# A decoder trunk on one core: new costs in the kernel's own scheduler, another load order in a pair, fewer warm-up matmuls

## The chip, the core and the metric

The kernel runs on one core of a Trainium2 chip. The metric is the device time of one execution in microseconds, median of the runs shown. The program is built in Python: it first plans the order of all its instructions on the host and then issues them in that order, each engine's queue in order. Only the time on the device counts.

## What is computed

A trunk of two decoder layers on 256 positions of width 1024, in float32. Each layer has a SwiGLU feed-forward block, a mixer (a chunkwise mLSTM in the first layer, differential attention on shared keys and values in the second), a second SwiGLU block and a gated input embedding; RMS norms stand around each of them. Cut to what matters:

```python
def reference(x, p, norm_g, w_ffn_in, w_ffn_out, ...):
    for layer in range(DEPTH):                      # 2
        g = norm_g[layer]
        h = swiglu(rms_norm(x, g[0]), w_ffn_in[layer, 0], w_ffn_out[layer, 0])
        x = x + 0.5 * rms_norm(h, g[1])
        h = rms_norm(x, g[2])
        h = mlstm_mixer(h, ...) if layer < N_A_LAYERS else diff_attention(h, k_sh, v_sh, ...)
        x = x + rms_norm(h, g[3])
        h = swiglu(rms_norm(x, g[4]), w_ffn_in[layer, 1], w_ffn_out[layer, 1])
        x = x + 0.5 * rms_norm(h, g[5])
        gate = jax.nn.sigmoid(rms_norm(x, g[6]) @ w_ple_gate[layer])
        x = x + rms_norm((p[layer] @ w_ple_proj[layer]) * gate, g[7])
        if layer == N_A_LAYERS - 1:
            k_sh, v_sh = shared_kv(x, kv_norm, w_kv)
    return x
```

`swiglu` is `(silu(gate) * up) @ w_out` with `gate, up = split(x @ w_in)`; its hidden width is 2816, worked on as 11 slices of 256 (`NJ`).

## The kernel before

**Arithmetic.** A float32 product is made from three products of TensorE's faster float32r type. `split` writes a high part of a tile with ScalarE (`activation` Copy to float32r) and the remainder with VectorE (`tensor_tensor` subtract); `mm3` then multiplies high by high, high by low and low by high. Weights arrive as raw tiles of 128 x 2048 float32, 1 MB each (`wraw`, 8 buffers), and are split into `whi` and `wlo` (6 buffers each). The 256 positions are two row tiles, t = 0 and 1.

**Pairs.** Within a feed-forward block some slices are taken two at a time (`PAIRS`, 15 pairs in all; one more is in the mLSTM). `block_pair` works out the 2 x 2 block product of (two row tiles) by (two slices) with seven block products in place of eight, in Strassen's manner, with sums and differences of weight tiles. Its function `load` issues a plain load on SP's queue and, for a sum, a second load on GpSimd's queue that adds into the same tile (`accum_op`). A pair takes seven transfers: `t3` (two), `u1` (two), `b11`, `b21` and `b22`. VectorE adds `b11 + t3` and `b21 + b11` (`add`, into the raw tiles). TensorE uses the parts in the order `w11`, `w21`, `wt2`, `wu1`, `wt3`, `w22`, `wt4`.

**The hidden chain.** For each slice and row tile `hidden` does a SiLU (ScalarE, tile `sg`), a product (VectorE, `h`), two transposes (TensorE, `tr`), and a split (`hh`, `hl`); `stage_out` multiplies the result with the output weights into `accO`. At the end of a block `post` forms the norm: squares on ScalarE (`waste`), two small operations on GpSimd (`sm`), then the update of `x` on VectorE.

**The planner.** The kernel is recorded twice. In the first recording `Notes.add` notes each operation with what it must follow; `Notes.cost` gives it `dur` (how long its engine is taken) and `lat` (when its result is there). `Notes.play` then plays the program event by event: it keeps a clock for each engine and, for each engine, chooses among the operations that could start first, by their rank (place in the program) and whether they are marked urgent (the splits of weights are not). Buffers of a tag are given out in program order as they become free. SP takes the lowest rank of those loads that have a buffer, with at most eight loads (`LANES`) in flight. The result, `self.order`, is the order in which the second recording issues everything (`issue`, line 389, which is why every row of the profile names L389). The chip's engines then run their queues in that fixed order and wait for what they need by semaphores; the planned times decide only the order.

For the costs before: a plain load begins 1.9 us after its issue, runs at 400 bytes a ns after the load before it, and is there 0.4 us later. An accumulating load begins 4 us after its issue, runs at 165 bytes a ns, holds up plain loads for the same time, and is there 4 us later. An operation of VectorE costs 155 ns beside its elements, one of ScalarE 200 (172 from PSUM), with the results 50 and 40 ns later.

**Start.** While the first loads are on their way, TensorE runs 12 matmuls on a zero tile (line 506).

## Time and profile before

| what | value |
|---|---|
| median of 3 runs | 1011.77 us |
| runs | 1009.74 to 1012.2 us |
| the profiled execution's own time | 1012.75 us |
| its span, first to last instruction | 1011.0 us |
| mean granted TensorE clock | 0.998 |
| moved by DMA | 262.11 MB, 259 GB/s over the span |

How to read the rows below. PE is TensorE's matmuls, PEld its weight loads, DVE VectorE, ACT ScalarE, POOL GpSimd and SP SyncE, which only issues loads; a q behind a name is the engine's sequencer. A group's row gives line, engine, operation, the tiles written and read (buffer numbers left out), the shape, the count, then busy time, mean ns of one, and idle time of the engine just before them with what ended it. In the timeline a row has start, duration, engine, operation, and in square brackets the idle time before it. The end of a matmul is modelled: neighbours overlap in the records, and the distance between two starts is the true pace.

### The profile page before, as it was taken

To read this page: it belongs to the slowest core of one execution; us is meant where nothing else is said; L and a number is where in the kernel's file an instruction comes from. 1 tells how busy PE (TensorE), PEld (TensorE's weight loads), DVE (VectorE), ACT (ScalarE), POOL (GpSimd) and SP (SyncE) were. 2 spreads that over 40 slices of the span, in tenths; PEclk is the share of its full clock that TensorE was granted. 3 is DMA by queue.
4 is the path that set the end of the run, shared out by engine and by line. 5 is a ranking of instruction groups with operands and counts; after the bars stand their busy time and mean duration, and the time that the engine had idled before them with its cause. 6 is when DMAs were issued, how large, how long until landed. Compare 5 with 4: busy or idle time off the path is not lost.

```text
span 1011.0 us, 12465 instructions
## 1 busy us (share of the span) xinstructions
PE 996.6 (99%) x4692; PEld 815.2 (81%) x4692; DVE 847.1 (84%) x886; ACT 674.3 (67%) x909; POOL 77.3 (8%) x118
## 2 busy tenths in 40 slices
PE   9999999999999999999999999999999999999997
PEld 7887787888878888888887888778778888888786
DVE  6999895888879899987888898986985899999783
ACT  7666683667657767656875677766866767768372
POOL 0000000100121000001110000000101200000010
PEclk9999999999999999999999999999999999999999
DMA  9999974955699788765779998784556997897631
GB/s 341 395 308 296 306 279 152 279 206 198 247 318 277 251 290 263 282 257 172 292 259 327 321 300 301 240 322 170 201 217 235 311 263 235 293 303 269 229 124 43
DMA packets 44132, 262.11 MB, mean 259 GB/s; under 512 B 5288, under 2 KB 5672, under 8 KB 15912
## 3 DMA queue, kind: packets, MB, share of 16 engines
q1 hardware_dynamic: 39176, 227.50, 58.7%
q0 software_dynamic: 4608, 33.56, 17.1%
q8 instruction: 37, 0.61, 0.2%
q10 hardware_dynamic: 288, 0.27, 0.1%
q14 instruction: 23, 0.19, 0.1%
HBM read 250.82 MB, written 10.49 MB: 258 GB/s over the span
## 4 chain that ended last, share of the span: by engine, by line
PE 83%; DMA 7%; DVE 6%; issue 2%; ACT 1%; POOL 0%; SPq 0%; DVEq 0%; POOLq 0%; ACTq 0%
PE accI L389 51%; PE accO L389 28%; DMA wraw<-in_ffn_in 5%; PE tr L389 4%; DVE wraw L389 1%; DVE wlo_4r L389 1%; DMA wraw<-in_x 1%; DVE wlo_3r L389 1%; DMA wraw<-in_xT 1%; DMA att<-in_diff_lambda 1%; DVE wlo_2r L389 1%; DVE wlo_1r L389 1%; DVE att L389 1%; DVE wlo_5r L389 0%; DVE sm L389 0%
## 5 line engine op out<-in xcount | busy, mean ns | idle before, releaser
L389 ACT ACTIVATE whi_0r<-wraw 128x2048 fp32r<-128x2048 f32 (+2 forms) x51 | 74.9, 1477 | 17.1 <-PE accI L389 4.9
L389 ACT ACTIVATE whi_1r<-wraw 128x2048 fp32r<-128x2048 f32 (+2 forms) x52 | 74.7, 1449 | 9.5 <-DMA wraw<-in_ffn_in 3.8
L389 ACT ACTIVATE whi_5r<-wraw 128x2048 fp32r<-128x2048 f32 (+1 forms) x49 | 72.6, 1493 | 9.5 <-DMA wraw<-in_ffn_in 2.5
L389 ACT ACTIVATE whi_2r<-wraw 128x2048 fp32r<-128x2048 f32 (+1 forms) x45 | 70.2, 1571 | 9.3 <-DMA wraw<-in_ffn_in 5.8
L389 ACT ACTIVATE whi_3r<-wraw 128x2048 fp32r<-128x2048 f32 (+1 forms) x47 | 72.2, 1546 | 5.4 <-PE accI L389 2.6
L389 ACT ACTIVATE whi_4r<-wraw 128x2048 fp32r<-128x2048 f32 (+1 forms) x44 | 69.8, 1599 | 8.5 <-DMA wraw<-in_ffn_in 3.4
L389 DVE TENSOR_TENSOR wraw<-wraw,wraw 128x2048 f32<-128x2048 f32 x32 | 73.0, 2282 | 0.1
L389 ACT ACTIVATE att<-accI 128x512 f32<-128x512 f32 x64 | 38.1, 596 | 27.1 <-PE accI L389 26.7
L389 POOL DMA_DIRECT2D wraw<-in_ffn_in x30 | 26.8, 893 | 370.6 <-DMA wraw<-in_ffn_in 287.2
L389 ACT ACTIVATE sg<-accI,sm 128x256 f32<-128x256 f32 x43 | 20.2, 470 | 41.4 <-PE accI L389 30.7
L389 DVE TENSOR_TENSOR wlo_4r<-wraw,whi_5r 128x2048 fp32r<-128x2048 f32 (+1 forms) x25 | 44.0, 1770 | 1.8 <-ACT whi_5r L389 1.8
L389 DVE TENSOR_TENSOR wlo_1r<-wraw,whi_0r 128x2048 fp32r<-128x2048 f32 (+1 forms) x25 | 43.9, 1771 | 1.5 <-ACT whi_0r L389 1.5
L389 DVE TENSOR_TENSOR wlo_5r<-wraw,whi_1r 128x2048 fp32r<-128x2048 f32 (+1 forms) x24 | 44.0, 1839 | 0.1
L389 POOL TENSOR_SCALAR sm<-sm 128x1 f32<-128x1 f32 x32 | 18.6, 582 | 327.3 <-ACT waste L389 327.2
L389 DVE TENSOR_TENSOR wlo_0r<-wraw,whi_0r 128x2048 fp32r<-128x2048 f32 (+2 forms) x24 | 41.8, 1751 | 2.0 <-ACT whi_0r L389 2.0
L389 DVE TENSOR_TENSOR wlo_2r<-wraw,whi_3r 128x2048 fp32r<-128x2048 f32 (+1 forms) x23 | 41.6, 1819 | 1.8 <-ACT whi_3r L389 1.8
L389 DVE TENSOR_TENSOR wlo_1r<-wraw,whi_1r 128x2048 fp32r<-128x2048 f32 (+2 forms) x26 | 42.0, 1626 | 1.1 <-ACT whi_1r L389 1.0
L389 DVE TENSOR_TENSOR wlo_3r<-wraw,whi_4r 128x2048 fp32r<-128x2048 f32 (+1 forms) x22 | 41.5, 1895 | 1.5 <-ACT whi_4r L389 1.5
L389 DVE TENSOR_TENSOR wlo_2r<-wraw,whi_2r 128x2048 fp32r<-128x2048 f32 (+1 forms) x22 | 41.5, 1896 | 1.0 <-ACT whi_2r L389 0.9
L389 DVE TENSOR_TENSOR wlo_4r<-wraw,whi_4r 128x2048 fp32r<-128x2048 f32 (+1 forms) x22 | 41.4, 1896 | 0.7 <-ACT whi_4r L389 0.7
L389 DVE TENSOR_TENSOR wlo_3r<-wraw,whi_3r 128x2048 fp32r<-128x2048 f32 (+1 forms) x22 | 41.5, 1895 | 0.4 <-ACT whi_3r L389 0.4
L389 DVE TENSOR_TENSOR wlo_0r<-wraw,whi_2r 128x2048 fp32r<-128x2048 f32 (+1 forms) x23 | 41.5, 1818 | 0.0
(488 smaller groups left out, 3033.7 us busy)
## 6 DMA issues: line engine op xcount, KB each, us to landing
wraw<-in_ffn_in SPq DMA_DIRECT2D x99, 1024.0 KB, 7.8
wraw<-in_ffn_out SPq DMA_DIRECT2D x44, 1024.0 KB, 10.2
wraw<-in_ffn_in POOLq DMA_DIRECT2D x30, 1024.0 KB, 11.8
wraw<-in_mlstm_in SPq DMA_DIRECT2D x13, 1024.0 KB, 4.8
wraw<-in_ple_gate SPq DMA_DIRECT2D x8, 1024.0 KB, 5.3
wraw<-in_w_kv SPq DMA_DIRECT2D x8, 1024.0 KB, 4.8
home<-wraw SPq DMA_DIRECT2D x28, 256.0 KB, 4.0
wraw<-home SPq DMA_DIRECT2D x14, 512.0 KB, 3.3
```

The lines of the kernel that those rows point to most:

```text
L389: getattr(getattr(self.nc, eng), name)(*args, **kw)
```

## The change

Three things change. In `cost` and `play` the constants and the model of transfers are others: VectorE's and ScalarE's operations take their engine for a shorter time with the result coming later by as much; plain and accumulating loads flow at the same time, plain ones at a third and accumulating ones at two thirds of their own rate while both are under way, and a later load may push back the planned landing of an earlier one; matmuls of 64 rows and of one column have costs of their own; and an operation that follows another one on its own engine is ready when the result is there, TensorE's excepted. In `block_pair` `b11` is loaded first, then `t3`, `b21` and `u1`. The warm-up has 8 matmuls. No arithmetic of the layers changes.

```diff
--- before.py
+++ after.py
@@ -214,27 +214,32 @@
         if o.name == "dma_start":
             size = math.prod(c for s, c in outs[0].ap) * 4
             o.dur = {"sync": 450, "scalar": 450, "gpsimd": 900}[o.eng]
-            o.lat = size / (165.0 if o.kw.get("accum_op") is not None else 400.0)
+            o.lat = size / (200.0 if o.kw.get("accum_op") is not None else 390.0)
         elif o.eng == "tensor":
             if o.name == "transpose":
                 o.dur, o.lat = 109, 310
             elif ins[0].dtype == F32R:
                 o.dur, o.lat = n / 2.4 + 14, n / 2.4 + 215
             else:
-                o.dur = max(n * 4 / 2.4 + 6, 70)
+
+                o.dur = max(n * 4 / 2.4 / (2 if ins[0].ap[0][1] == 64 else 1) + 6, 70 if n * 4 < P else 105)
+                if n == 1:
+                    o.dur = 210
                 o.lat = o.dur + 270
         elif o.eng == "scalar":
             ptr = any(k in o.kw and isinstance(o.kw[k], bass.AP) for k in ("scale", "bias"))
-            o.dur = 0.83 * m + (200 if sb_in else 172) + (90 if ptr else 0)
-            o.lat = o.dur + (110 if o.kw.get("accum_out") is not None else 0) + 40
+
+            sums = o.kw.get("accum_out") is not None
+            o.dur = 0.83 * m + (100 if sb_in else 72) + (90 if ptr else 0) + (90 if sums else 0)
+            o.lat = o.dur + (110 if sums else 0) + 140
             f = o.args[2] if len(o.args) > 2 else None
             o.table = f if f in (AF.Silu, AF.Exp, AF.Ln, AF.Sigmoid) else None
         elif o.eng == "vector":
             one = o.name in ("tensor_copy", "tensor_scalar", "memset") and len(sb_in) == len(ins)
-            o.dur = m / 0.96 / (2 if one else 1) + 155 + (60 if o.name == "scalar_tensor_tensor" else 0)
+            o.dur = m / 0.96 / (2 if one else 1) + 70 + (60 if o.name == "scalar_tensor_tensor" else 0)
             if o.name == "tensor_tensor_scan":
-                o.dur = 680
-            o.lat = o.dur + 50
+                o.dur = 600
+            o.lat = o.dur + 135
             o.two = len(sb_in) > 1
         elif o.eng == "gpsimd":
             o.dur = 560 if o.name == "tensor_tensor" else 320 + m
@@ -278,6 +283,8 @@
                 t = turn[tag].pop(0)
                 given[t] = when
                 self.slot[t] = slot
+                return t
+            return None
 
         for tag in turn:
             for i in range(self.bufs[tag]):
@@ -287,8 +294,35 @@
         for o in ops:
             if not o.left:
                 waiting[o.eng].append(o)
-        dma_free = add_free = 0.0
+
+        flow = {False: [], True: []}
+        flow_at = 0.0
         landed = []
+        freed = {}
+
+        def step(queues, t, until, done):
+            while t < until:
+                act = [k for k in queues if queues[k] and queues[k][0][0] <= t]
+                share = {k: 1.0 if len(act) == 1 else (1 / 3, 2 / 3)[k] for k in act}
+                stop = min([until] + [t + queues[k][0][1] / share[k] for k in act]
+                           + [q[0][0] for k, q in queues.items() if q and k not in act])
+                for k in act:
+                    queues[k][0][1] -= (stop - t) * share[k]
+                    if queues[k][0][1] < 1e-6:
+                        done(queues[k].pop(0)[2], stop)
+                t = stop
+                if not any(queues.values()):
+                    break
+
+        def later(q, t):
+            t += 400
+            if t > q.end:
+                q.end = t
+                for u in q.users:
+                    if u.start is None and u.after[q]:
+                        u.ready = max(u.ready, t)
+                for v in freed.get(q, ()):
+                    given[v] = max(given[v], t)
         lock_until = 0.0
         before = "r"
         table = AF.Silu
@@ -311,7 +345,7 @@
                     w = place(o)
                     if w is not None:
                         if o.name == "dma_start" and e != "gpsimd" and len(landed) >= LANES:
-                            w = max(w, landed[-LANES])
+                            w = max(w, landed[-LANES].end)
                         cands.append((max(w, clock[e]), o, w))
                 if not cands:
                     continue
@@ -337,18 +371,15 @@
             waiting[e].remove(o)
             o.start = s
             if o.name == "dma_start":
-                if o.kw.get("accum_op") is None:
-                    begin = max(s + 1900, dma_free)
-                    dma_free = begin + o.lat
-                    o.end = dma_free + 400
-                    if e != "gpsimd":
-                        landed.append(o.end)
-                else:
-
-                    begin = max(s + 4000, add_free)
-                    add_free = begin + o.lat
-                    dma_free = max(dma_free, begin) + o.lat
-                    o.end = add_free + 4000
+                adds = o.kw.get("accum_op") is not None
+                o.end = s
+                if s > flow_at:
+                    step(flow, flow_at, s, lambda q, t: None)
+                    flow_at = s
+                flow[adds].append([s + (2600 if adds else 1700), o.lat, o])
+                step({k: [list(q) for q in v] for k, v in flow.items()}, flow_at, 1e12, later)
+                if e != "gpsimd":
+                    landed.append(o)
                 clock[e] = s + o.dur
             else:
                 end = s + o.dur
@@ -369,7 +400,7 @@
             for u in o.users:
                 u.left -= 1
                 if u.after[o]:
-                    u.ready = max(u.ready, o.end if u.eng != e or o.name == "dma_start" else clock[e])
+                    u.ready = max(u.ready, o.end if u.eng != "tensor" or e != u.eng else clock[e])
                     if u.eng != e:
                         u.far = max(u.far, o.end)
                 else:
@@ -380,7 +411,9 @@
                 last[t][0] -= 1
                 last[t][1] = max(last[t][1], o.end)
                 if not last[t][0]:
-                    give(self.tag_of[t], self.slot[t], last[t][1])
+                    v = give(self.tag_of[t], self.slot[t], last[t][1])
+                    if v and o.name == "dma_start":
+                        freed.setdefault(o, []).append(v)
         self.order = [i for o in order for i in o.parts]
 
     def issue(self):
@@ -503,7 +536,7 @@
     wz = T([P, P], "h", 2)
     nc.vector.memset(wz, 0.0)
     warm = trp()
-    for i in range(12):
+    for i in range(8):
         nc.tensor.matmul(warm[:, :P], wz, wz, start=True, stop=True)
 
 
@@ -673,12 +706,12 @@
             return parts(out)
 
         nc.is_urgent = False
+        b11 = load(src[0])
         t3 = load(src2[0], src2[1])
-        u1 = load(src[0], src2[0])
-        b11 = load(src[0])
         w11 = parts(b11)
         b21 = load(src[1])
         w21 = parts(b21)
+        u1 = load(src[0], src2[0])
         wt2 = add(b11, b11, t3)
         wu1 = parts(u1)
         wt3 = parts(t3)
```

## The prediction

> **What bounds the kernel now.** I read the page's head and its chain of waits first. The second of the rows below gives each engine's busy time, the third the chain by engine.
>
> ```profile
> span 1011.0 us, 12465 instructions
> PE 996.6 (99%) x4692; PEld 815.2 (81%) x4692; DVE 847.1 (84%) x886; ACT 674.3 (67%) x909; POOL 77.3 (8%) x118
> ...
> PE 83%; DMA 7%; DVE 6%; issue 2%; ACT 1%; POOL 0%; SPq 0%; DVEq 0%; POOLq 0%; ACTq 0%
> ```
>
> TensorE is the bound: 996.6 of 1011.0 us. The change removes no matmul from the layers; what it can give back is TensorE's idle time, 14.4 us. Next I cut the span into stretches (columns: stretch, length, busy time of PE, PEld, DVE, ACT and POOL with counts, clock, DMA share, GB/s).
>
> ```profile
> 1.04:6.18 5.14, 5.14 (x24) 5.14 (x25) 1.44 (x3) 2.30 (x4) 0.32 (x2) 1.00 0.81 244
> 6.18:100.00 93.82, 93.23 (x419) 75.96 (x419) 82.02 (x81) 66.64 (x81) 6.33 (x9) 1.00 0.99 346
> 100.00:125.00 25.00, 23.83 (x108) 19.40 (x107) 21.93 (x18) 16.10 (x17) 1.21 (x2) 1.00 0.96 313
> ...
> 275.00:300.00 25.00, 24.00 (x112) 19.60 (x112) 17.79 (x22) 13.40 (x23) 4.38 (x7) 1.00 1.02 308
> ...
> 525.00:550.00 25.00, 23.65 (x109) 18.96 (x108) 20.33 (x24) 13.00 (x16) 0.87 (x1) 1.00 0.99 306
> 550.00:725.00 175.00, 174.35 (x804) 142.23 (x803) 153.10 (x140) 121.79 (x147) 12.08 (x16) 1.00 0.79 272
> 725.00:775.00 50.00, 48.77 (x301) 39.39 (x300) 40.53 (x72) 37.37 (x101) 3.11 (x3) 1.00 0.59 222
> ...
> 1003.63:1011.00 7.37, 0.00 (x0) 0.00 (x0) 2.26 (x4) 0.98 (x3) 0.85 (x2) 0.75 0.19 71
> ```
>
> TensorE's idle time is 0.59, 1.17, 1.00, 1.35, 0.65 and 1.23 us in rows two to seven: 6.0 us. The rest is 1.04 us ahead of the first matmul and a tail of 7.37 us. The tail is one chain of dependent operations after the last matmul and has nothing to reorder. So 6.0 us, and a little hidden in matmul ends that are modelled, is all that a better order can recover. Who causes it? The timeline around two of the stalls (start, duration, engine, operation, and in brackets idle time and what ended it):
>
> ```profile
> 113.22 1.92 ACT L389 ACTIVATE whi_4r<-wraw 128x2048 fp32r<-128x2048 f32 x1 [3.44 <-DMA wraw<-in_ffn_in]
> ...
> 120.96 0.44 PE L389 MATMUL tr<-ident,h 128*128 128x128 f32 x2 [1.17 <-DVE hl_2r L389]
> ...
> 546.47 1.92 ACT L389 ACTIVATE whi_2r<-wraw 128x2048 fp32r<-128x2048 f32 x1 [3.85 <-DMA wraw<-in_ffn_in]
> ...
> 548.85 0.48 DVE L389 SCALAR_TENSOR_TENSOR h<-accI,sm,sg 128x256 f32<-128x256 f32 x1 [1.82 <-ACT sg L389]
> ...
> 549.39 0.44 PE L389 MATMUL tr<-ident,h 128*128 128x128 f32 x2 [1.27 <-DVE h L389]
> ```
>
> ScalarE's queue is in order. It held a weight split whose tile landed 3.4 to 3.9 us later than the planner thought; the SiLU queued behind it came late, so did `h`, and TensorE stood for 1.2 us. Another kind of stall, at a layer's end:
>
> ```profile
> 283.47 0.95 POOL L389 DMA_DIRECT2D wraw<-in_ffn_in  x1 [15.36 <-DMA wraw<-in_ffn_in]
> ...
> 286.64 0.86 POOL L389 DMA_DIRECT2D wraw<-in_ffn_in  x1 [2.23 <-ACT waste L389]
> 287.59 0.30 POOL L389 TENSOR_SCALAR sm<-sm 128x1 f32<-128x1 f32 x1
> ...
> 289.39 0.66 PE L389 MATMUL tr<-ident,wraw 128*128 128x128 f32 x4 [1.00 <-DVE wraw L389]
> ```
>
> GpSimd issues an accumulating load (0.86 us) just ahead of the norm's two small operations; the transposes that need that norm wait 1.00 us.
>
> **The change part by part. Transfers.** Rows: two queues (packets, MB, share of 16 engines' span), and issues with median us to landing, the last two in the stretches 845.8 to 847 and 524 to 533 us.
>
> ```profile
> q1 hardware_dynamic: 39176, 227.50, 58.7%
> q0 software_dynamic: 4608, 33.56, 17.1%
> ...
> wraw<-in_ffn_in SPq DMA_DIRECT2D x99, 1024.0 KB, 7.8
> ...
> wraw<-in_ffn_in POOLq DMA_DIRECT2D x30, 1024.0 KB, 11.8
> ...
> wraw<-in_ffn_in POOLq DMA_DIRECT2D x1, 1024.0 KB, 8.0
> ...
> wraw<-in_ffn_in POOLq DMA_DIRECT2D x2, 1024.0 KB, 12.4
> ```
>
> Plain loads moved 227.5 MB in 0.587 x 1011 = 593 us, 383 GB/s; accumulating ones 33.56 MB in 173 us, 194 GB/s. The new constants (390 and 200) fit, the old (400 and 165) less. For a 1.05 MB accumulating load alone the old cost says 4.0 + 6.36 + 4.0 = 14.4 us, the new one 2.6 + 5.24 + 0.4 = 8.2; the trace has 8.0. The old plan was too gloomy on these and, as the two ScalarE waits show, too hopeful on plain loads beside them; the new plan gives a plain load a third of the rate there. I expect it to put the SiLU ahead of a split that will land late. Of the 1.17 + 1.35 us in the two stretches I take 2.2 as recovered (bounds: 0, since the new order may meet another late tile; 2.5, all of it).
>
> **Overlap on VectorE and ScalarE.** Four rows of the timeline:
>
> ```profile
> 61.65 2.28 DVE L389 TENSOR_TENSOR wraw<-wraw,wraw 128x2048 f32<-128x2048 f32 x1
> ...
> 63.85 2.28 DVE L389 TENSOR_TENSOR wlo_1r<-wraw,whi_1r 128x2048 fp32r<-128x2048 f32 x1
> ...
> 61.44 1.92 ACT L389 ACTIVATE whi_1r<-wraw 128x2048 fp32r<-128x2048 f32 x1 [1.09 <-DVE wraw L389]
> ...
> 63.26 1.90 ACT L389 ACTIVATE whi_2r<-wraw 128x2048 fp32r<-128x2048 f32 x1
> ```
>
> The second operation starts 2.20 us after the first on VectorE, 1.82 on ScalarE, each before the first's recorded end. The new costs (2048/0.96 + 70 = 2203 ns; 0.83 x 2048 + 100 = 1800 ns) are the pitch; the old (2288 and 1900) the duration. Total latency stays (155 + 50 = 70 + 135). The Trainium skill, "VectorE: DVE Perf Modes", section "The DRAIN you can't avoid", says that after each operation the next does not start until the pipeline has emptied; by it the old cost would be right and the new plan would run some 85 ns an operation ahead of the chip. The two VectorE rows contradict it by 0.08 us, so I give this edit no loss. The correction is 4% on a large operation and mostly moves all of an engine's queue together: 0 us, bounds -1 and +1 (both engines have idle time, 164 and 337 us by the second row above).
>
> **Cheaper small matmuls.** From the groups of the differential attention and of the mLSTM denominators:
>
> ```profile
> L389 PE MATMUL accO<-wraw,wraw 64*128 64x128 f32 x96 | 6.6, 282 | 0.0
> ...
> L389 PE MATMUL tr<-sg,att 128*128 128x1 f32 x24 | 2.8, 243 | 0.0
> ```
>
> Each planned matmul appears as two rows. 48 score matmuls took 6.6 us, 0.14 each; the old cost is 0.22 each (10.5 in all), the new 0.11 (5.4). 12 one-column ones took 0.23 each; old 0.07, new 0.21. In the attention the old plan held TensorE busy 3.9 us longer than it is, so its order has TensorE arrive early and wait for the softmax (in the mLSTM it was 1.9 us too short). Of the 1.23 us idle in the stretch from 725 to 775 I take 1.0 as recovered (bounds 0 and 1.23).
>
> **First tile first.** Per pair the same seven transfers, in the order `b11`, `t3`, `b21`, `u1` for `t3`, `u1`, `b11`, `b21`; 15 feed-forward pairs and one in the mLSTM. SP issues the same loads; the second accumulating load on GpSimd's queue comes after one more plain load has been asked for. TensorE uses `w11`, `w21`, `wt2`, `wu1` in that order, so the new order is that of use, and the splits that ScalarE is asked for first land before any accumulate competes. `b11` and `b21` hold their buffers longer by two and one loads, `u1` shorter by two. The accumulating load that stands in front of the norm at 286.64 us is the second of its pair (the first was issued at 283.47, ahead of the wait); pushed later it leaves the norm alone: 0.9 recovered of 1.00 (bounds 0 and 1.0). The smaller stalls (0.59 and 0.65) have both causes; I take 0.6 of 1.24.
>
> **Eight warm-up matmuls.** Rows: TensorE's first matmuls and three pieces of the chain of waits.
>
> ```profile
> 1.04 5.49 PE L389 MATMUL tr<-h 128*128 128x128 f32 x24 [1.04 <-DVE h L389]
> ...
> 4.25 0.63 ACT L389 ACTIVATE whi_0r<-wraw 128x512 fp32r<-128x512 f32 x1 [1.11 <-DMA wraw<-in_ffn_in]
> ...
> 7.18 0.42 PE L389 MATMUL accI<-wlo_0r,xh_0r 128*128 128x512 f32 x1
> 7.45 0.40 PE L389 MATMUL accI<-whi_0r,xl_0r 128*128 128x512 f32 x1
> ...
> 9.51 7.82 DMA wraw<-in_x
> ...
> 19.94 0.46 ACT sg L389
> ...
> 20.97 0.50 PE accI L389
> ```
>
> Twelve take 1.04 to 6.18, 0.43 us each; eight end at 4.46, and the first real matmul waits for its weight split until about 4.9 (4.25 + 0.63) in place of 6.18. But nothing of that reaches the end: the chain goes through the load of `x` (landing at 17.33), its norm and the first SiLU to a matmul at 20.97, which has TensorE idle just before it. So 0 us; bound below: -0.4, what the idle there was. The matmuls start at half speed (0.43 a warm-up, 0.23 from 7.45 on).
>
> **The sum**: 2.2 + 1.0 + 0.9 + 0.6 = 4.7 us recovered. Against it: the old plan's 14.4 us kept VectorE from ever waiting for an accumulate; with 8.2 planned and 12.4 seen beside other loads it will wait sometimes. I take +0.7 for it (bounds 0 and the rival below). Net -4.0: span 1007.0. The profiled execution took 1012.75 us, 1.75 over its span, and 0.98 over the median of 1011.77: 1007.0 + 1.75 - 0.98 = **1007.8**.
>
> **Rivals. The stalls only move** (time 1011.8). TensorE is filled to 99%, the new plan is another greedy order, and whatever it still misjudges makes stalls elsewhere. For it: six idle stretches with three different causes. Against: two of the causes are constants that the rows above contradict.
>
> **VectorE waits for accumulates** (slower, 1016.7). The group of the sums in section 5 of the page (count, busy, mean ns, idle ahead of them):
>
> ```profile
> L389 DVE TENSOR_TENSOR wraw<-wraw,wraw 128x2048 f32<-128x2048 f32 x32 | 73.0, 2282 | 0.1
> ```
>
> Place: these 32 sums, which read an accumulated tile or follow it in VectorE's queue; `h` and `hl` stand behind them, and TensorE's transposes behind those. Price: waits of 3.44 and 3.85 us on ScalarE cost TensorE 1.17 and 1.27, so a wait pays from about 2.4 us on and costs 1.2 when it is 3.5. If eight of the 32 land that late, 8 x 1.2 = 9.6 against the 4.7 recovered: +4.9 on the span, 1011.77 + 4.9 = 1016.7. For it: an idle of 0.1 us says that the old plan never tried how early they can go, and an accumulate takes 8.0 us alone but 12.4 beside plain loads, planned at most at 10.9 (two thirds of the rate). Against: that gap is 1.5 us, under the 2.4.
>
> **The clock stays low for longer** (1008.5). Low speed lasted from 1.04 to about 7.2 us. With a pause from 4.46 to 4.9 the count may start anew: low speed to 4.9 + 6.1 = 11.0, 14 real matmuls at 0.43 by then, against about 19 before; five behind at 0.23 is 1.1 us, less the 0.4 of idle at 20.97: +0.7. The Trainium skill, "TensorE: Matmul & The Clock Gate", section "What's actually happening", states that the full clock comes after about 3.4 us of sustained activity in a window that runs freely; eight warm-ups of 0.43 are just that long. The trace agrees with it only loosely: 6.1 us here.
>
> **How the numbers follow.** Forecast 0.55, its own range 1003.5 to 1010 (all 6 us and what the modelled ends hide, down to 2 us); stalls only move 0.25; accumulates 0.16; clock 0.04. About 0.3% (3.0 us) is what a measurement can tell from no change, so the bound for faster is 1008.7. Faster: 0.47 of the forecast and 0.03 of the clock case, 0.50. Same: 0.08 + 0.25 + 0.01 = 0.34. Slower: 0.16. The range 1003.5 to 1014 leaves out the slower rival and a little below.
>
> **What would show it.** TensorE's idle time between first and last matmul at about 2 us; no ScalarE wait for `wraw<-in_ffn_in` above 3 us ahead of a SiLU; no accumulating issue directly ahead of a norm on GpSimd; less idle from 725 to 775 us. VectorE's group `wraw<-wraw,wraw` with some us of idle ended by DMA, where it had almost none, would show the price. I am wrong if the recovered stalls come back under other names, or if that last group waits for tens of us.

## The result, and the profile after

The changed kernel took **1026.89 us** (median of four executions) against 1010.75 us before (1008.73 to 1012.2) on the same chip: slower, ratio 1.0148, interval 1.0098 to 1.0197. One of the four, of 1243.28 us, which was also the profiled one, had TensorE at a mean granted clock of 0.752; the ratio goes by the other three, 1022.82 to 1029.45 us, and the rows of "the changed kernel" below are of a second profile of the same kernel, an execution of 1023.96 us at a clock of 0.995 (median of its series 1024.64, ratio 1.0149). The forecast was 1007.8 with a range to 1014.0.

The head of that page: span, and busy time of each engine.

```profile
span 1022.2 us, 12498 instructions
...
PE 997.6 (98%) x4684; PEld 814.1 (80%) x4684; DVE 844.4 (83%) x886; ACT 672.2 (66%) x909; POOL 80.2 (8%) x118
```

TensorE's work is what it was (997.6 us against 996.6); the span grew by 11.2. The same stretch in both, from the first matmul to the end of the last, shows where. First the changed kernel (columns as in the prediction's stretches):

```profile
1.04:1014.80 1013.76, 997.61 (x4684) 814.11 (x4684) 841.95 (x881) 671.18 (x906) 78.89 (x110) 1.00 0.76 258
```

Then the kernel before:

```profile
1.04:1003.63 1002.59, 996.59 (x4692) 815.21 (x4692) 844.68 (x881) 673.27 (x906) 76.02 (x111) 1.00 0.77 261
```

TensorE's idle time went from 6.0 to 16.15 us, and its busy time up by 1.0. Head and tail are the same. So the 6.0 us that the prediction set out to recover were not recovered; 10.1 us came on top. The list of waits of the changed kernel says for what (us in total, times, longest):

```profile
PE tr L422 <- DVE hl_0r L422: 9.5, 3, 6.0
PE tr L422 <- DVE hl_2r L422: 2.7, 2, 1.5
PE tr L422 <- DVE h L422: 2.6, 3, 1.0
...
ACT whi_3r L422 <- DMA wraw<-in_ffn_in: 9.9, 3, 6.6
ACT whi_1r L422 <- DMA wraw<-in_ffn_in: 4.6, 2, 3.5
ACT whi_5r L422 <- DMA wraw<-in_ffn_in: 4.2, 2, 2.6
```

In the list of before (below), TensorE waited 4.7 us in all for `h` and its parts and for a norm, and ScalarE's longest wait for a feed-forward tile was 3.9:

```profile
PE tr L389 <- DVE h L389: 2.5, 3, 1.3
PE tr L389 <- DVE hl_2r L389: 1.2, 1, 1.2
...
PE tr L389 <- DVE wraw L389: 1.0, 1, 1.0
...
ACT whi_2r L389 <- DMA wraw<-in_ffn_in: 5.8, 4, 3.9
```

In all, ScalarE waited no longer for the tiles of `in_ffn_in` than before (21.5 us by its whole list, against 21.2), but the single waits grew. The pattern begins as before: ScalarE holds a split whose tile is late, and the hidden chain stands behind it. The largest case, in the timeline of the changed kernel:

```profile
841.76 0.89 POOL L422 DMA_DIRECT2D wraw<-in_ffn_in  x1 [12.99 <-DMA wraw<-in_ffn_in]
...
854.06 0.39 PE L422 MATMUL accO<-whi_5r,hh_1r 128*128 128x512 f32 x1
855.12 1.91 ACT L422 ACTIVATE whi_3r<-wraw 128x2048 fp32r<-128x2048 f32 x1 [6.61 <-DMA wraw<-in_ffn_in]
856.93 0.46 ACT L422 ACTIVATE sg<-accI,sm 128x256 f32<-128x256 f32 x1
857.29 1.90 ACT L422 ACTIVATE whi_4r<-wraw 128x2048 fp32r<-128x2048 f32 x1
857.42 0.48 DVE L422 SCALAR_TENSOR_TENSOR h<-accI,sm,sg 128x256 f32<-128x256 f32 x1 [6.19 <-ACT sg L422]
...
859.09 0.37 ACT L422 ACTIVATE hh_0r<-tr 128x256 fp32r<-128x256 f32 x1
...
860.02 0.42 DVE L422 TENSOR_TENSOR hl_0r<-tr,hh_0r 128x256 fp32r<-128x256 f32 x1
...
860.49 0.69 PE L422 MATMUL tr<-ident,h 128*128 128x128 f32 x2 [6.04 <-DVE hl_0r L422]
860.83 0.77 PE L422 MATMUL accO<-whi_5r,hh_1r 128*128 128x512 f32 x1
```

Behind the late split ScalarE's queue holds the SiLU, then a second weight split (`whi_4r`), and only then `hh_0r`, the split of the transposes that had been done before the stall. The tile `tr` has one buffer, so TensorE's next transposes wait until `hh_0r` and `hl_0r` have read it. That ends the stall, not the SiLU with its `h`; of the list's first three rows 12.2 us stand under `hl` and 2.6 under `h`. Four waits of ScalarE above 2.5 us end this way: 2.57, 2.89, 3.54 and 6.61 us of waiting are followed by stalls of TensorE of 2.01, 1.53, 1.48 and 6.04 us, 11.1 of the 16.15.

The DMA issues of 841 to 842.5 us give that load's time to landing:

```profile
wraw<-in_ffn_in POOLq DMA_DIRECT2D x1, 1024.0 KB, 13.3
```

841.8 + 13.3 = 855.1: the split starts on the tile in the moment it lands. Why it stands there can be read from the plan: the planner runs on the host and gives the same plan each time, so its own time for every operation can be set beside the trace's. At this place the chip runs 16.1 us behind the plan. The plan has the load land at 832.38 us of its own clock and starts the split in that same moment. The last row shows a second price: the matmul is recorded with 0.77 us, where the one ahead of the stall, in the same group, has 0.39. The stretches around it:

```profile
850.00:857.50 7.50, 4.45 (x20) 3.35 (x18) 1.31 (x2) 2.38 (x3) 0.00 (x0) 1.00 0.71 232
857.50:864.30 6.80, 3.81 (x10) 3.12 (x11) 6.02 (x6) 5.09 (x5) 0.00 (x0) 0.50 0.45 160
864.30:870.00 5.70, 5.70 (x27) 4.66 (x26) 5.70 (x3) 1.99 (x3) 0.87 (x1) 1.00 0.99 266
```

From 857.5 us on, still within the stall, the granted clock was 0.50 for 6.8 us: 3.81 us busy at half speed, 1.9 us lost. The Trainium skill, "TensorE: Matmul & The Clock Gate", section "What's actually happening", describes a window of about 3.4 us that runs freely and takes the clock down after one that was idle; the trace agrees here: the 6.8 us are two of these, and the window before them, from 854.1, holds a single matmul (a case with more work in its window follows below).

Why was the tile late? It is `u1` of a pair, and the lateness came down a chain of transfers that begins with the stores of `x`. In the issues of 792 to 811 us, beside accumulating loads, these took

```profile
home<-wraw SPq DMA_DIRECT2D x4, 256.0 KB, 8.5
```

and in those of 974 to 993, where no accumulating load runs,

```profile
home<-wraw SPq DMA_DIRECT2D x4, 256.0 KB, 2.0
```

Against the plan's times, moved by the 16.1 us: the store issued at 810.67 us took 8.9 us in place of 5.5 and gave its buffer free 3.3 us late. The plain load of `t3` takes that buffer and was issued 3.5 us late, its accumulate 3.8. The plain load of `u1`, issued on time, shared the way with that late accumulate and took 10.3 us in place of 6.9; so the accumulate of `u1` was issued 4.1 us late, and it took 13.3 us itself, where the plan had 10.9. 4.1 and 2.4 are the wait of 6.6. No transfer was more than 3.5 us over its plan; the excess added up from one to the next, and the plan had 0.4 us of room for it. The chip's median for these loads is also over the plan's longest, 10.9 us beside plain loads all the way:

```profile
wraw<-in_ffn_in POOLq DMA_DIRECT2D x30, 1024.0 KB, 12.5
```

### The profile page after: what moved, and what is told of

Its sections match the earlier page's. It is cut to its first block, busy times and chain, and to the rows that moved or that the text cites. A ratio compares the mean times of both kernels' runs of the same rounds, so it can differ in the third digit from the quotient of the medians.

```text
span 1241.5 us, 12498 instructions
## 1 busy us (share of the span) xinstructions
PE 1232.9 (99%) x4684; PEld 879.1 (71%) x4684; DVE 854.8 (69%) x886; ACT 677.7 (55%) x909; POOL 80.2 (6%) x118
## 4 chain that ended last, share of the span: by engine, by line
PE 99%; DMA 0%; DVE 0%; ACT 0%; issue 0%; DVEq 0%; POOLq 0%; POOL 0%; ACTq 0%
PE accI L422 63%; PE accO L422 31%; PE tr L422 4%; DMA wraw<-in_ffn_in 0%; DVE wraw L422 0%; DVEq L1430 0%; ACT whi_0r L422 0%; POOLq L1430 0%; ACT att L422 0%; DVE att L422 0%; DVE hl_1r L422 0%; ACT waste L422 0%; POOL sm L422 0%; ACTq L1430 0%; POOLq L422 0%
## 5 line engine op out<-in xcount | busy, mean ns | idle before, releaser
L422 DVE TENSOR_TENSOR att<-accI,att 128x512 f32<-128x512 f32 x32 | 22.1, 690 | 36.5 <-PE accI L422 36.2
L422 ACT ACTIVATE att<-accI,sm 128x512 f32<-128x512 f32 (+1 forms) x25 | 16.8, 672 | 53.2 <-PE accI L422 51.1
L422 ACT ACTIVATE waste<-accO 128x512 bf16<-128x512 f32 (+2 forms) x46 | 20.3, 446 | 45.4 <-PE accO L422 42.3
```

What stands on the lines that cost most here:

```text
L422: getattr(getattr(self.nc, eng), name)(*args, **kw)
```

## The experiments

My theory, the landings: the new plan takes a landing at what it holds for the mean time, with 400 ns to spare; where the old one gave an accumulating load 14.4 us alone, it gives 8.2, and tiles land behind the operations that wait for them at the head of ScalarE's and VectorE's queues. The rivals: the load order alone (the accumulate of `u1` now comes last); the engines' costs; the warm-ups and the clock. In the tables "idle" is what TensorE's busy time leaves of the stretch from the first to the end of the last matmul, as in the two rows above; "at once" is how many of the 32 accumulated tiles had their first ScalarE or VectorE operation within 0.2 us of landing (time of issue plus time to landing, against that operation's start); "half clock" is the time, in us, at a granted clock of 0.5 between head and tail. A blank was not worked out. Each kernel's time stands beside that of before in the same series (1011.2 to 1011.8 us).

### The parts alone: warm-ups, load order

The changed kernel again, and with twelve warm-ups; the kernel before with eight; the kernel before with the new load order.

```diff
-    for i in range(8):
+    for i in range(12):
```

> The changed kernel once more, for a profile at full clock. Its profile so far was taken at a granted clock of 0.752 throughout, its other runs at 0.992 to 0.994 against 0.998 before. If the loss is in the kernel and not in that one execution: 1022 to 1030 us again. Theory O (the new order thins TensorE's work at some places, so that its clock is halved for windows of 3.4 us, as the slow profile shows once after 16 one-column matmuls): two to four such windows in the clock rows, 1.7 us lost in each, and stalls of 5 to 10 us beside them. Theory W (the shorter warm-up lets the clock be opened to less than full at the start): a clock under 1.00 in the first 20 us or throughout. Theory L (the new load order): full clock and idle time of TensorE at the pairs, ended by DMA or by the sums of weight tiles.

> The changed kernel with 12 warm-up matmuls again, nothing else undone. O: no better than the changed kernel, 1020 to 1030 us. W: back to about 1008 to 1012 us with a clock of 0.998. L: as O.

> The kernel before with 8 warm-up matmuls and nothing else changed. O and L: within 3 us of before (1008 to 1014 us). W: 1015 us or more, or some runs at a granted clock of about 0.75.

```diff
+        b11 = load(src[0])
         t3 = load(src2[0], src2[1])
-        u1 = load(src[0], src2[0])
-        b11 = load(src[0])
         w11 = parts(b11)
         b21 = load(src[1])
         w21 = parts(b21)
+        u1 = load(src[0], src2[0])
```

> The kernel before with the new load order in a pair and nothing else changed. L: 1018 us or more, with idle time of TensorE at the pairs. O and W: within 4 us of before, 1007 to 1015 us.

```
                                median us  ratio [95%]              span    idle   at once  half clock
before                          1011.3     1                        1011.0   6.0    1        0
changed                         1024.64    1.0149 [1.0097, 1.0201]  1022.2  16.2   12       6.8
changed, 12 warm-ups            1025.18    1.0142 [1.0112, 1.0171]  1022.8  14.9            6.8
before, 8 warm-ups              1010.78    0.9992 [0.9974, 1.0009]  1009.7   6.2             0
before, new load order          1021.40    1.0101 [1.0067, 1.0135]  1016.7   8.0    3       6.8
```

The warm-up rival falls: they do nothing in either kernel. The load order holds for a good part: alone it costs 10 us with the old costs, and not through waits for tiles. Its stretches in the mLSTM layer:

```profile
221.00:226.40 5.40, 3.65 (x20) 2.61 (x18) 4.56 (x11) 5.37 (x9) 0.00 (x0) 1.00 0.54 194
226.40:233.20 6.80, 6.69 (x16) 4.74 (x16) 3.48 (x9) 3.88 (x6) 0.00 (x0) 0.50 0.00 0
```

and of the kernel before at that place:

```profile
222.00:227.00 5.00, 5.00 (x26) 3.82 (x25) 3.94 (x9) 4.23 (x8) 0.00 (x0) 1.00 0.60 210
227.00:234.00 7.00, 7.00 (x33) 5.29 (x34) 5.70 (x14) 6.01 (x10) 0.00 (x0) 1.00 0.00 0
```

Here the mLSTM's small matmuls wait on one another through ScalarE and VectorE, and large products of the pair had filled the gaps. With the new order fewer were left: TensorE was busy 3.65 of 5.40 us, then the clock halved for 6.8 us. Idle (1.75) and half of the busy 6.69 (3.35) are 5.1 of this execution's 5.7 us. That leaves some 4 us of the median's 10 that this profile does not hold. Most of the price stands in the plan already: with the new order the end of the old planner's own plan (the landing of its last store) moves from 1001.9 to 1009.4 us, and it has TensorE idle at this same place (1.25 and 1.35 us). So with the old costs the load order costs time before any tile is late.

### The costs alone

The engines' costs and ready rule in the kernel before; the transfers' model in the kernel before; all new costs with the old load order and twelve warm-ups; and the changed kernel with the accumulates' planned landing 3 us later. The first three take the front's diff by hunks: `cost` (but for its DMA line) with the rule for `u.ready`; the DMA line of `cost` with `flow`, `step`, `later`; and both.

> The kernel before with the new costs of the engines' operations alone (and the rule that a follower on the same engine waits for the result); transfers, load order and warm-up as before. Theory P (the new plan lets an accumulated tile land too early, puts its split on ScalarE ahead of a SiLU, and TensorE waits): no part of it is in here, 1008 to 1013 us. Theory L (the load order costs it): the same. Theory E (the shorter times of VectorE and ScalarE make the plan run ahead of the chip): 1016 us or more, with stalls ended by VectorE.

> The kernel before with the new model of transfers alone; costs of the engines, load order and warm-up as before. P: 1016 us or more, ScalarE waits of 2 to 6 us for wraw<-in_ffn_in with a TensorE stall 1 to 2 us shorter behind each. L and E: 1007 to 1013 us.

> All new costs with the old load order and 12 warm-ups, so the changed kernel without its load order. L: 1006 to 1012 us, the 10 us of the load order gone. P: 1016 us or more, as in the changed kernel. If both hold in part, 1012 to 1016.

```diff
-            t += 400
+            t += 400 if q.kw.get("accum_op") is None else 3400
```

> The changed kernel with one number of its plan changed: an accumulating load is taken to land 3.4 us after its last byte in place of 0.4, so 11.2 us alone in place of 8.2. P: the ScalarE wait of 6.6 us at 855 us and most of the TensorE stalls of over 1 us ahead of tr<-ident,h are gone, no clock window at half there, 1014 us or less. L: as the changed kernel, 1020 us or more.

```
                                median us  ratio [95%]              span    idle   at once  half clock
engine costs alone              1016.21    1.0039 [1.0024, 1.0053]  1012.5   6.0            3.4
transfer model alone            1018.54    1.0058 [1.0044, 1.0072]  1014.6   8.7             0
all costs, old order            1015.09    1.0038 [1.0019, 1.0056]  1014.4   6.4    3       6.8
changed, accumulates +3 us      1019.52    1.0076 [1.0050, 1.0103]  1021.9  10.7    3      13.6
```

Each half of the costs costs something by itself, 4.4 and 6.8 us over 1011.77, and together 3.3: they do not add. The load order on top of all costs is again 10 us (1025.18 - 1015.09, both with twelve warm-ups), but not in the same way: with the new costs the plans of both orders end at 997.1 us, so the plan sees nothing of this loss. Later landings of accumulates took nine of the twelve "at once" away, but 5 us of the time and not the 13: the theory as stated, about accumulates, is too narrow, and its forecast of 1014 us or less was missed. In the kernel with the engines' costs alone the wait is for a plain load's tile:

```profile
629.57 1.91 ACT L394 ACTIVATE whi_3r<-wraw 128x2048 fp32r<-128x2048 f32 x1 [3.51 <-DMA wraw<-in_ffn_in]
...
632.02 0.50 PE L394 MATMUL accI<-whi_1r,xh_1r 128*128 128x512 f32 x1 [2.52 <-ACT att L394]
```

A wait of 3.51 cost TensorE 2.52 us, and behind it came 3.4 us at half clock. Its idle time, 6.0, is that of before, so this one profile holds 1.5 us of loss (the half clock's) where the median has 4.4.

### The load orders, and a margin on every landing

Which step of the order costs? Three orders; and, for a wider theory, that every landing is planned too tightly, a margin on the landing of both kinds of loads (1.4 us for plain ones, 4.0 for accumulates) with all new costs.

```diff
-        u1 = load(src[0], src2[0])
         w11 = parts(b11)
+        u1 = load(src[0], src2[0])
```

This is the first, in the changed kernel: `b11, t3, u1, b21`. The others are `t3, b11, b21, u1` and `b11, t3, u1, b21` in the kernel before.

> The changed kernel with the loads of a pair in the order b11, t3, u1, b21: u1 is asked for one place earlier, ahead of b21 as it was before; b11 stays first. Theory U (the loss of the load order is u1: it takes a plain load and then an accumulate, some 20 us in all, and asked for last it lands when its split is due): close to all new costs with the old load order, 1012 to 1018 us, few accumulated tiles that land under 0.2 us before their first use. Theory B (the loss is b11 first, whose buffer is held longest): 1020 us or more.

> The kernel before with only u1 moved behind b21: t3, b11, b21, u1. U: 1018 to 1024 us, all of what the new load order cost there (1021.4). B: 1008 to 1014 us.

> The kernel before with only b11 moved to the front: b11, t3, u1, b21. U: 1008 to 1014 us. B: 1018 to 1024 us.

```diff
-            t += 400
+            t += 1400 if q.kw.get("accum_op") is None else 4000
```

> All new costs, the old load order, 12 warm-ups, and a margin in the plan: loads land 1 us, accumulates 3.6 us later than the new model says. Theory P (what the new costs lose, 3.3 us, are tiles that land later than planned with a SiLU behind them on ScalarE): 1006 to 1012 us, the TensorE stalls of over 2 us at 82 and 540 us gone. If the margin only moves the stalls: 1013 to 1018.

```
                                median us  ratio [95%]              span    idle   at once  half clock
changed, b11 t3 u1 b21          1022.62    1.0102 [1.0067, 1.0137]  1017.8  12.6    8        0
before, t3 b11 b21 u1           1024.08    1.0120 [1.0088, 1.0151]  1022.4  11.8           10.2
before, b11 t3 u1 b21           1018.86    1.0069 [1.0045, 1.0094]  1017.6   9.4            6.8
all costs, old order, margin    1009.77    0.9981 [0.9961, 1.0001]  1007.9   3.3    2        0
```

With the old costs both steps hurt: `u1` last costs 12.9 us, `b11` first with `u1` third 7.7. In the changed kernel, putting `u1` ahead of `b21` again gained only 2.0 us, inside the intervals, where theory U had forecast 1012 to 1018 us; so the place of `u1` is not the whole of it. `t3` and `u1` are each a plain load with an accumulate on top, so they need the longest lead (7 + 12 us by the medians of issue to landing); `b11` first takes lead from both, and the new order gives `u1` the shortest. That the loss goes by lead, and not by buffers that are held longer, is argued and not separated here. The margin took the loss of the costs away, 1015.09 to 1009.77.

### The margin in the changed kernel

The same margin with everything else as changed; a larger one (1.9 and 5.4) with the old order; and, as a control, later plain landings in the old model.

> The changed kernel, its new load order and 8 warm-ups kept, with the margin that made all new costs good in the old load order (loads 1 us, accumulates 3.6 us later in the plan; 1009.8 us there). If the loss of the load order is only that the plan believes tiles too early: 1008 to 1013 us. If the load order takes away time that accumulated tiles need, whatever the plan believes (theory U, widened: t3 and u1 must be asked for ahead of b11 and b21): 1015 to 1022 us, with TensorE stalls or windows of half clock left.

```diff
-            t += 400
+            t += 1900 if q.kw.get("accum_op") is None else 5400
```

> All new costs, old load order, 12 warm-ups and a larger margin: loads 1.5 us, accumulates 5 us later. If late tiles make what is left of the stalls (5.0 us, the largest at 82 and 869 us behind ScalarE waits of 2.2 and 2.5 us): 1005 to 1009 us. If the margin is large enough already: 1008 to 1012.

```diff
-                    o.end = dma_free + 400
+                    o.end = dma_free + 1400
```

> The kernel before, old costs and old load order, with plain loads taken to land 1 us later in the plan. If a margin is what counts, whatever the costs: 1006 to 1010 us, the stalls at 119 and 548 us gone. If the margin pays only with the new costs, because the old ones already overstate accumulates and serialise transfers, and more of it delays work for nothing: 1012 to 1022 us.

Then the larger margin in the changed kernel, and a margin on plain loads alone (1.4 and 0.4).

> The changed kernel (new load order, 8 warm-ups) with the larger margin: loads 1.5 us, accumulates 5 us later in the plan. Theory P (all of the change's loss is tiles that land later than planned): 1005 to 1010 us, under before. If the new load order has a price of its own that the margin of 1 and 3.6 us happened to hide: 1011 us or more.

> The changed kernel with the margin on plain loads alone: 1 us later in the plan, accumulates as the new costs have them. With the margin on accumulates alone it was 1019.5 us. If the accumulates' margin is the larger part: 1017 to 1023 us. If a plain load that lands late is what counts (it also sets when its accumulate may be issued): 1009 to 1014 us.

```
                                median us  ratio [95%]              span    idle   at once  half clock
changed, margin 1.4/4.0         1009.71    0.9984 [0.9968, 0.9999]  1007.1   3.4    3        0
old order, margin 1.9/5.4       1007.09    0.9950 [0.9934, 0.9965]  1006.2   3.2    1        0
before, plain loads +1 us       1027.76    1.0150 [1.0118, 1.0181]  1025.7  12.3           17.0
changed, margin 1.9/5.4         1006.50    0.9950 [0.9923, 0.9977]  1004.5   1.1    0        0
changed, margin 1.4/0.4         1020.38    1.0094 [1.0077, 1.0111]  1018.2  11.0   13       3.4
```

Two numbers in one line of `later` turn the changed kernel from 13.3 us slower into 5.0 us faster than before, with its load order, its costs and its eight warm-ups as they are. Neither kind of landing is enough alone: accumulates alone (3.4, not 4.0) gave 1019.52, plain loads alone 1020.38, both together 1009.71. The plans show what each margin leaves. Counted are the loads into `wraw`, as far as the trace gives their landing, that took over 1 us longer from issue to landing than their plan says:

```
                                plain       accumulating  median us
changed                         34 of 202   24 of 32      1024.64
changed, accumulates +3 us      49 of 202    1 of 32      1019.52
changed, margin 1.4/0.4          9 of 203   24 of 32      1020.38
changed, margin 1.4/4.0         11 of 202    0 of 32      1009.71
changed, margin 1.9/5.4          2 of 201    0 of 32      1006.50
```

In the eleven profiles with the new model of transfers, the four with at most 13 such loads of both kinds belong to kernels of 1006.5 to 1009.8 us, the seven with 33 or more to kernels of 1015.1 to 1025.2; within the seven the count gives no order. The load order, 10 us without a margin, costs nothing with it (1009.71 against 1009.77; 1006.50 against 1007.09). The control went the other way: the same extra microsecond on plain loads in the old model cost 16 us, so these runs show "later is better" only with the model that lets both kinds of transfers flow at once. In the old model the plan itself gets longer, from 1001.9 to 1013.9 us by its own end, so most of that loss is not one of late tiles; why the plan gets so much longer was not followed further.

The page and the waits of the changed kernel with the margin of 1.9 and 5.4, which beats both kernels:

```profile
span 1004.5 us, 12491 instructions
...
PE 994.9 (99%) x4684; PEld 812.8 (81%) x4684; DVE 842.7 (84%) x886; ACT 674.8 (67%) x909; POOL 80.8 (8%) x118
...
PE tr L422 <- DVE h L422: 1.0, 1, 1.0
PE accI L422 <- DVE h L422: 0.2, 1, 0.2
...
ACT whi_0r L422 <- DMA wraw<-in_ffn_in: 1.1, 1, 1.1
ACT whi_2r L422 <- DMA wraw<-in_ffn_in: 1.0, 2, 0.8
```

The 1.0 us is the start, ahead of the first matmul. TensorE waits for nothing else beyond 0.2 us, and ScalarE's longest wait for a feed-forward tile is 1.1. The stretch from first to last matmul:

```profile
1.04:997.00 995.96, 994.82 (x4684) 812.80 (x4684) 840.29 (x881) 673.86 (x906) 79.44 (x110) 1.00 0.77 263
```

1.1 us idle in place of 6.0 before and 16.15 in the changed kernel.

## Why the prediction was wrong, step by step

- **TensorE is the bound, and only its idle time can move**: right, in every kernel. The prediction's bound on the gain (6 us and a little) held too: the best version found has 1.1 us idle, and its span is 6.5 us shorter.
- **Transfers** (2.2 us recovered, +0.7 for waits): this step failed. The rates were right, and so was an accumulating load alone (8.0 us against 8.2). Beside plain loads the plan had it land too early: at most 10.9 us planned, a median of 12.5 measured, 1.6 us over the plan in the mean of all 32. The prediction had seen this gap, 12.4 against 10.9, and put it aside as 1.5 us, under the 2.4 that a wait must pass before it costs anything; it counted one load, and along a chain of transfers the excess became 6.6. The step "I expect it to put the SiLU ahead of a split that will land late" does not follow either: a plan without room puts the split first whenever the landing runs over. The old plan's 14.4 us, which the prediction called too gloomy, were that room: its accumulating loads landed 4.0 us sooner after their issue than planned, in the mean. 12 of 32 accumulated tiles were used at once in place of 1, ScalarE's longest wait grew from 3.9 to 6.6 us, and TensorE's idle time by 10.1 us. With room on both kinds of landings the 2.2 us, and more, did come.
- **The rival "VectorE waits for accumulates"** came nearest: late accumulates, at a cost to TensorE. Three things were wrong in it. It waits on the wrong engine: the split on ScalarE, with the SiLU, another split and `hh` behind it, is what costs; VectorE's waits for feed-forward tiles were 3.9 us in all, the row below. Its price was too low: it held waits up to 2.4 us for free and one of 3.5 for 1.2; a wait of 2.57 us cost 2.01 of idle, and the one of 6.6 cost 6.0 and 1.9 of half clock. And what it put against itself, the gap of 1.5 us, was one link of a chain. It said 1016.7; the kernel took 1024.6 to 1026.9.

```profile
DVE wraw L422 <- DMA wraw<-in_ffn_in: 3.9, 2, 2.3
```

- **First tile first** (0.9 and part of 0.6 recovered): failed. The argument was the order of use on TensorE; it left out the lead that `t3` and `u1` need, each a load with an accumulate on top. The order cost 10 us with the old costs and 10 with the new, and nothing once the plan had a margin. The stall at the norm in front of GpSimd's accumulate did go, but not shown by this cause: it was gone with all new costs in the old order too, and with `b11, t3, u1, b21` TensorE waited 0.8 us (changed kernel) and 1.3 us (old costs) for a norm.
- **Overlap on VectorE and ScalarE** (0, bounds -1 and +1): the engines' costs alone gave +4.4 us (interval 2.4 to 5.4 by the ratio), outside the bounds; that run also holds the cheaper small matmuls and the ready rule, so how much of it is the overlap stays open. The pitch was read rightly from the rows. That a 4% shift "moves all of an engine's queue together" leaves out that it moves the queue against the landings of tiles; the wait of 3.51 us at 629.57 is the one case of it that was looked at.
- **Cheaper small matmuls** (1.0 recovered): right for the stretch, and with the right cause as far as the runs part it. From 720 to 785 us, around the differential attention, the changed kernel idles 0.2 us, where 1.23 were idle before. With the engines' costs alone no idle is left from 10 us ahead of these matmuls to 20 us behind them; with the transfers' model or the load order alone 1.2 and 0.8 us are. Which of the engines' costs did it is not parted. The stretch in the changed kernel:

```profile
720.00:785.00 65.00, 64.80 (x391) 53.47 (x390) 49.91 (x85) 46.29 (x124) 3.43 (x4) 1.00 0.58 218
```

- **Eight warm-ups** (0): right, 0.9992 [0.9974, 1.0009]. The rival of the low clock was put at the wrong place: the clock falls in the middle of the kernel, after stalls.
- **The range**: its upper end came from the forecast and "stalls only move", and left the slower rival out. A plan with less room should have given it more weight. The planner's own end had promised the gain: 997.1 us for the changed kernel against 1001.9, 4.8 less, near the 4.0 forecast; its promise holds only as far as tiles land as planned.

What stays open: why the old planner's plans get longer by 7.4 us with the new load order and by 12.0 with later plain landings; and which step of the load order costs what in the changed kernel without a margin. That the late stores of `x` began the chain at 855 us is read from the trace and the plan, and was not tried by itself. The kernel before may owe something to a lucky order: six of seven edits of it alone cost 4.4 to 16.5 us. The margins are not open to this doubt in the same way, as all four kernels with a margin on both kinds of landings are at or below it.

## What to carry to other kernels

When a planner's cost of a transfer is corrected to the mean that the trace shows, ask what its old excess was paying for. In an in-order queue a tile that lands late holds everything behind it, and lateness adds up from transfer to transfer; room in the plan cost little here: the plan with the largest margin ends 4.1 us later by its own reckoning than the one without (1001.2 against 997.1) and ran 18.1 us faster. So plan landings at the mean plus their spread (here 1.9 us on plain and 5.4 on accumulating loads, 1006.5 us against 1024.6 with 0.4). Set the plan's own end beside the time on the chip: where both get worse, look for the loss in the plan, and where only the chip does, in the costs. A load order has to be judged by the lead that each tile needs, and not only by the order of use. Look at the longest waits first: ScalarE's waits had nearly the same sum before and after, and a single stall of TensorE of 2 us or more can cost a halved clock besides.

## What the hardware showed that was not expected

- The clock halves in the middle of a kernel, for 3.4, 6.8 or 10.2 us, around single TensorE stalls of 2.0 to 6.0 us or after thin work (3.65 of 5.40 us busy in the mLSTM). Not every such stall did it: one of 2.02 us did (changed, accumulates +3 us, at 553.5), and ones of 2.91 us (transfer model alone, at 541.4) and 2.86 us (changed, margin 1.4/0.4, at 857.8) passed without. The lengths are multiples of the 3.4 us that the Trainium skill, "TensorE: Matmul & The Clock Gate", section "What's actually happening", gives for its window. A stall of 2.0 us cannot fill one, which goes beyond the page; whether it counts may depend on where in a window it falls, which was not tried.
- A 1 MB accumulating load landed after 8.0 us alone and 12 to 13 beside plain loads (medians); stores of 256 KB after 2.0 us where no accumulating load ran and 8.5 beside one (medians of four).
